# One-hot product for the last queries, merged indices and a more cautious order search in a threshold-attention kernel

## The chip, the cores and the metric

The kernel runs on one core of a Trainium2 chip. The metric is the device time of one launch in microseconds (us), of which lower is better. A run also records its span (first to last instruction of the core) and the mean clock that was granted to TensorE. The calls for runs fell on different chips; the runs of one call share a chip.

## The reference

```python
Q, K, V: (8, 12, 512, 64) float32, normal draws; threshold = 0.1
scores  = einsum('bhqd,bhkd->bhqk', Q, K) / sqrt(64)
weights = softmax(scores)                              # max subtracted, + 1e-10
weights = where(weights > threshold, weights, 0)
weights = weights / (weights.sum(-1) + 1e-10)
out     = einsum('bhqk,bhkd->bhqd', weights, V)
```

With these inputs few rows have a weight above 0.1, and those have one. Such a row of the output is one row of V; all others are zero.

## The kernel before

The output is filled with zeros. All scores are computed once in 16 bits and only **screened** (an exponential with a sum on ScalarE, or a maximum on VectorE) for rows that could hold a weight above 0.1. The few candidates of each group of four heads are then numbered, gathered, multiplied again in FP32 and judged exactly; the row of V is gathered and scattered into the output. There are 24 groups, g0 to g23. A guard sends inputs that do not fit to a general path, which these inputs never take.

```python
def do_qk(g):                     # 16-bit scores, one bank of PSUM for each head
    ...
        keep(nc.tensor.matmul(sc[:], lhsT=qk[ps, 0, hp % 2, r * P:(r + 1) * P],
                              rhs=qk[ps, 1, hp % 2, :], start=True, stop=True))
def do_screen(g, h2):
    ...
    if (h2, r) in ACT_TILES[tiles_of(q)]:
        nc.scalar.activation(junk[:], sc[:], ACTF.Exp, scale=BETA * scale / CS, accum_out=at)
    else:
        nc.vector.tensor_reduce(at, sc[:], axis=AX.X, op=ALU.max)

def do_rank(q):                   # 16 short size matmuls (for the guard), then the count of flags
    for n in range(2):
        for which in range(2):
            for r in range(SO):
                c = (1 + which) * KEY + n * C2 + 2 * r
                size = sq[:, which, n, r * P:(r + 1) * P]
                keep(nc.tensor.matmul(rk[:, c:c + 2], lhsT=size.bitcast(bf16) if which else size,
                                      rhs=heads[which][:], start=True, stop=True))
    ...                           # 8 more short matmuls with tri and ones
# then, each stage waiting for the one before:
#   keys -> one-hot (do_onehot) -> row numbers by matmul (do_idx) -> gather of Q rows ->
#   split by head -> transpose -> FP32 product (do_xqk) -> exponential -> pick -> indices ->
#   gather of V rows -> scatter to the output

def do_xone(q):
    one = small.tile([P, 1], f32)
    keep(nc.vector.tensor_scalar(one[:], kept[:, q:q + 1], ALONE, 0.0, op0=ALU.add, op1=ALU.max))
    vidx = small.tile([P, 1], i32)
    keep(nc.vector.tensor_scalar(vidx[:], one[:], 1024.0, T["rows", q][:, 3:4], op0=ALU.mult, op1=ALU.add))
    ...
def do_spare(n):                  # matmuls of nothing, in TensorE's gaps
    for _ in range(n):
        keep(nc.tensor.matmul(spare_ps[:], lhsT=warm[:, 0:P], rhs=warm[:], start=True, stop=True))
```

The order of all these steps is searched when the kernel is built. `Schedule` holds a model with a duration for each step; a random search (with a fixed seed) changes priorities, and each order is judged by the mean of four simulated runs with a little jitter:

```python
def search(self, rounds, most):
    rnd = random.Random(1)
    def price(prios):
        ...
        self.order()
        self.fill()                                   # puts spare matmuls into TensorE's gaps
        return sum(self.run(seed)[0] for seed in range(4)) / 4
    ...
sched = Schedule({"sc": SC, "sm": SM}, {"gather": 3.2, "vgather": 3.2}, 3.0, SPARE)
for op, way, spare in sched.search(800, 1.0):
    do_spare(spare)
    op[4](way[0]) if len(op[1]) > 1 else op[4]()
```

The softmax here doesn't subtract the row's maximum and nothing guards it: scores larger than these inputs give would overflow.

## Time and profile before

| | |
|---|---|
| time, median of 3 runs (range) | 251.56 us (251.01 to 252.52) |
| the profiled run: time, span, clock | 233.99 us, 232.3 us, 0.974 |
| busy: ScalarE, VectorE, TensorE | 195.7, 200.6, 205.3 us |
| last screening ends, last scatter is issued | 209.70, 225.94 us |

The row of the page that gives the granted TensorE clock in 40 equal slices (a digit is tenths of full speed) shows a run that was nearly always at full clock:

```profile
PEclk9999999999999999999997999999999999999975
```

There is one dip in the body, a window at half clock from 121.3 us, and then only the tail, where little is left for TensorE.

### The profile page before, as it was taken

Reading aid. Unit: us, or ns where it says so; the run is one execution under the profiler, and the core shown is the slowest. Engines: PE = TensorE matmul, PEld = TensorE weight load, DVE = VectorE, ACT = ScalarE, POOL = GpSimd, SP = SyncE. Lnnn points to the kernel's source line nnn. Section 1 sums busy time; section 2 is a strip of 40 time slices with the busy share of each in tenths; the row PEclk is TensorE's granted clock in tenths of the full one; section 3 lists DMA queues with packets and bytes.
Section 4 is the critical chain, followed back from the end, with each engine's and each line's share of the span. In section 5 each row is a group of like instructions: output and inputs, shape, how many; then the busy total and the mean of one; then the engine's idle time right before and its main releaser. Section 6 shows DMA issues by size and latency. Waiting matters only on the chain. (4 is left out here: it accounts for less than half of the span.)

```text
span 232.3 us, 6061 instructions
## 1 busy us (share of the span) xinstructions
PE 205.3 (88%) x1997; PEld 101.9 (44%) x2026; DVE 200.6 (86%) x574; ACT 195.7 (84%) x651; POOL 102.8 (44%) x112
## 2 busy tenths in 40 slices
PE   6999999999999799999979899999989998999700
PEld 2454553645445254444534444455535454244200
DVE  4688998999999799999987999999999999994620
ACT  2899999999998799998996998999999998992300
POOL 8120331554523633825363635344641556357440
PEclk9999999999999999999997999999999999999975
DMA  6999899496795569784954895668795300000000
GB/s 133 229 204 282 246 159 297 75 178 213 143 219 135 108 119 278 116 181 138 176 123 76 187 206 164 97 162 217 137 318 231 49 4 9 2 5 11 2 5 0
DMA packets 70737, 32.72 MB, mean 141 GB/s; under 512 B 55442, under 2 KB 67552, under 8 KB 70704
## 3 DMA queue, kind: packets, MB, share of 16 engines
q1 hardware_dynamic: 54144, 25.17, 39.7%
q0 software_dynamic: 14448, 6.61, 22.5%
q10 hardware_dynamic: 2112, 0.52, 1.2%
q8 instruction: 17, 0.28, 0.5%
q14 instruction: 16, 0.13, 0.2%
HBM read 26.74 MB, written 13.37 MB: 173 GB/s over the span
## 5 line engine op out<-in xcount | busy, mean ns | idle before, releaser
L502 ACT ACTIVATE junk<-sc 128x512 bf16<-128x512 f32 x244 | 144.1, 619 | 4.0 <-PE sc L488 3.2
L504 DVE TENSOR_REDUCE stat<-sc 128x1 f32<-128x512 f32 x140 | 93.5, 683 | 5.1 <-PE sc L488 4.7
L488 PE MATMUL sc<-qk 64*128 64x512 f16 x384 | 69.1, 384 | 4.5 <-ACT junk L502 1.8
L502 ACT ACTIVATION_READ_ACCUMULATOR junk<-sc 128x1 f32 x244 | 56.0, 229 | 0.0
L667 PE MATMUL spare_ps<-warm 128*128 128x512 bf16 x151 | 46.2, 394 | 3.2 <-DVE warm L350 2.2
L636 POOL DMA_INDIRECT out_dram<-vsel,oidx x24 | 25.9, 1078 | 52.1 <-DVE stat L504 13.9
L629 POOL DMA_INDIRECT vsel<-in_V_dram,vidx x24 | 26.8, 1118 | 25.8 <-DVE vidx L620 13.9
L563 POOL DMA_INDIRECT qsel<-in_Q_dram,idx x24 | 26.6, 1107 | 26.2 <-DVE idx L553 18.5
L488 PEld LDWEIGHTS <-qk 64*128 64x128 f16 x384 | 16.2, 93 | 36.4 <-issue 31.1
L431 PE MATMUL sc<-identity_f,k_sb 128*128 128x128 f32 x192 | 30.8, 284 | 1.5 <-ACT junk L502 0.9
L455 ACT ACTIVATE kt<-sc 128x512 f32<-128x512 f32 x48 | 29.9, 625 | 2.1 <-PE sc L431 1.9
L667 PEld LDWEIGHTS <-warm 128*128 128x128 bf16 x180 | 16.2, 102 | 29.4 <-issue 22.0
L285 POOL DMA_DIRECT2D qh<-in_Q_dram x23 | 19.1, 831 | 19.3 <-PE sc L446 15.0
L593 PE MATMUL sc<-kt,xq 128*64 128x512 f32 x96 | 26.8, 636 | 0.4 <-DVE flags L508 0.2
L472 DVE TENSOR_SCALAR qk<-kt,ksum 128x512 f16<-128x512 f32 x48 | 24.1, 501 | 3.2 <-ACT kt L455 3.2
L431 PEld LDWEIGHTS sc<-identity_f,k_sb 128*128 128x128 f32 x192 | 21.1, 142 | 11.5 <-ACT junk L502 4.4
L600 ACT ACTIVATE e<-sc 128x512 f32<-128x512 f32 x24 | 14.7, 614 | 9.2 <-PE sc L593 9.0
L547 PEld LDWEIGHTS <-oh 128*128 128x128 f16 x192 | 14.1, 164 | 10.0 <-issue 4.2
L612 DVE SCALAR_TENSOR_TENSOR pick<-e,tv,worth 128x512 f32<-128x512 f32 x24 | 17.9, 747 | 0.2
L478 DVE TENSOR_SCALAR sq<-qk 128x2048 uint16<-128x2048 uint16 x24 | 16.8, 700 | 0.0
L547 PE MATMUL sm<-row_no,oh 128*128 128x4 f16 x192 | 15.4, 202 | 1.2 <-DVE oh L536 0.5
L536 DVE TENSOR_TENSOR oh<-slot_no,keys 128x1024 f16<-128x1024 bf16 x24 | 16.4, 683 | 0.1
(75 smaller groups left out, 187.5 us busy)
## 6 DMA issues: line engine op xcount, KB each, us to landing
out_dram<-zero SPq DMA_DIRECT2D x24, 512.0 KB, 5.7
k_sb<-in_K_dram SPq DMA_DIRECT2D x94, 128.0 KB, 4.3
qh<-in_Q_dram POOLq DMA_DIRECT2D x23, 256.0 KB, 4.8
qsel<-in_Q_dram,idx POOLq DMA_INDIRECT x24, 2.7
vsel<-in_V_dram,vidx POOLq DMA_INDIRECT x24, 3.5
out_dram<-vsel,oidx POOLq DMA_INDIRECT x24, 2.6
k_sb<-in_K_dram ACTq DMA_DIRECT2D x2, 128.0 KB
first<-in_Q_dram ACTq DMA_DIRECT2D x2, 128.0 KB, 5.2
```

The costliest lines, as they stand in the source:

```text
L431: keep(nc.tensor.matmul(sc[:, r * P:(r + 1) * P], lhsT=src[:, r, :], rhs=identity_f32[:], is_transpose=True, start=True, stop=True))
L455: ins = nc.scalar.activation(kt[:], sc[:], ACTF.Copy, accum_out=ksum[:])
L472: keep(nc.vector.tensor_scalar(T["qk", hp // 2][:, 1, hp % 2, :], T["kt", hp][:], CS, T.pop(("ksum", hp))[:, 0:1], op0=ALU.mult, op1=ALU.s ...
L488: keep(nc.tensor.matmul(sc[:], lhsT=qk[ps, 0, hp % 2, r * P:(r + 1) * P], rhs=qk[ps, 1, hp % 2, :], start=True, stop=True))
L502: keep(nc.scalar.activation(junk[:], sc[:], ACTF.Exp, scale=BETA * scale / CS, accum_out=at))
L504: keep(nc.vector.tensor_reduce(at, sc[:], axis=AX.X, op=ALU.max))
L547: keep(nc.tensor.matmul(ix[:], lhsT=oh[:, c, :], rhs=row_no[:, c, :], start=(c == 0), stop=(c == C2 - 1)))
L563: keep(nc.gpsimd.indirect_dma_start(out=qsel_bufs[q % NS][:], out_offset=None, in_=Qr, in_offset=bass.IndirectOffsetOnAxis(ap=T.pop(("idx" ...
L593: keep(nc.tensor.matmul(sc[sl, :], lhsT=xq[:, sl], rhs=T.pop(("kt", 2 * q + n))[:], start=True, stop=True))
L629: keep(nc.gpsimd.indirect_dma_start(out=vsel_bufs[q % NS][:], out_offset=None, in_=Vr, in_offset=bass.IndirectOffsetOnAxis(ap=T.pop(("vidx ...
L636: s = nc.gpsimd.indirect_dma_start(out=Or, out_offset=bass.IndirectOffsetOnAxis(ap=T.pop(("oidx", q))[:, 0:1], axis=0), in_=vsel_bufs[q % ...
L667: keep(nc.tensor.matmul(spare_ps[:], lhsT=warm[:, 0:P], rhs=warm[:], start=True, stop=True))
```

## The change

It has four parts. The indices of the V gather and the scatter are merged into one VectorE operation each. For the last group alone, a one-hot matrix in FP32 and matmuls against Q rows already in SBUF take the place of the gather of Q. The search judges an order by ten jittered runs instead of four, with later landings and 1200 rounds instead of 800. And the tile for the spare matmuls is set first. The intent: less VectorE work, a shorter tail, and an order that bears delays better.

```diff
-    def run(self, seed=None, late=0.02, drift=1.0):
+    def run(self, seed=None, late=0.05, drift=1.2):
-            return sum(self.run(seed)[0] for seed in range(4)) / 4
+            return sum(self.run(seed)[0] for seed in range(10)) / 10
+    warm = consts.tile([P, SO * P], bf16)                     # moved up from further down
+    keep(nc.vector.memset(warm[:], 0.0))
-    ALONE = 8192.0
+    ALONE = 2.0 ** 23
     ...
     def do_onehot(q):
+        if q == NQ - 1:
+            oh = lpool.tile([P, C2, 2, SLOTS], f32, name="oh_last")
+            keep(nc.vector.tensor_tensor(out=..., in0=slot_no..., in1=keys..., op=ALU.is_equal))
+            T["oh", q] = oh
+            return
     def do_idx(q):
-            keep(nc.tensor.matmul(ix[:], lhsT=oh[:, c, :], rhs=row_no[:, c, :],
+            keep(nc.tensor.matmul(ix[:], lhsT=oh[:, c, :], rhs=(row_no_f32 if q == NQ - 1 else row_no)[:, c, :],
+    def do_xsel(q):
+        ...
+        for n in range(2):
+            for r in range(SO):
+                for h2 in range(2):
+                    keep(nc.tensor.matmul(xp[h2 * D:(h2 + 1) * D, n * SLOTS:(n + 1) * SLOTS],
+                                          lhsT=last_q[n][:, r, h2 * D:(h2 + 1) * D], rhs=oh[:, h2 * SO + r, n, :],
+                                          start=(r == 0), stop=(r == SO - 1)))
+        ...
     def do_xone(q):
-        keep(nc.vector.tensor_scalar(one[:], kept[:, q:q + 1], ALONE, 0.0, op0=ALU.add, op1=ALU.max))
-        keep(nc.vector.tensor_scalar(vidx[:], one[:], 1024.0, T["rows", q][:, 3:4], op0=ALU.mult, op1=ALU.add))
+        keep(nc.vector.tensor_scalar(vidx[:], kept[:, q:q + 1], T["rows", q][:, 3:4], 0.0, op0=ALU.add, op1=ALU.max))
     ...
-    sched = Schedule({"sc": SC, "sm": SM}, {"gather": 3.2, "vgather": 3.2}, 3.0, SPARE)
+    sched = Schedule({"sc": SC, "sm": SM}, {"gather": 4.0, "vgather": 4.0}, 3.0, SPARE)
-    FAR, NEAR = 6.0, 4.3
+    FAR, NEAR = 7.0, 4.5
     ...                                     # POOL steps 1.1-1.2 -> 1.3, scatter landing 3.0 -> 4.0
-        stage("idx", IDX, ["oh"], do_idx, takes=[("sm", ("ix", q))])
+        stage("idx", IDX, ["oh"] if q < NQ - 1 else ["oh", "xsel"], do_idx, takes=[("sm", ("ix", q))])
-    for op, way, spare in sched.search(800, 1.0):
+    for op, way, spare in sched.search(1200, 1.0):
```

More of the change, by code (lines that the diff above doesn't have):

```diff
@@ L279 @@
     hpool = ctx.enter_context(tc.tile_pool(name="h", bufs=2))
+    lpool = ctx.enter_context(tc.tile_pool(name="last", bufs=1))
+    last_q = {}
     fpool = ctx.enter_context(tc.tile_pool(name="first", bufs=1))
@@ L322 @@
     nc.gpsimd.iota(row_i[:], pattern=[[S, 2], [1, SO]], base=-4 * S, channel_multiplier=SO)
+    row_no_f32 = consts.tile([P, C2, 4], f32)
     row_no = consts.tile([P, C2, 4], f16)
@@ L328 @@
     nc.gpsimd.tensor_copy(row_no[:, :, 0], row_i[:])
+    nc.gpsimd.tensor_copy(row_no_f32[:], row_no[:])
+    ALONE = 2.0 ** 23
     slot_base = consts.tile([P, 4], f32)
@@ L333 @@
     nc.vector.memset(slot_base[SLOTS:P, 0:1], float(6 * S))
-    nc.vector.memset(slot_base[SLOTS:P, 3:4], float(2 * S))
-    ALONE = 8192.0
+    nc.vector.memset(slot_base[0:SLOTS, 3:4], ALONE)
+    nc.vector.memset(slot_base[SLOTS:P, 3:4], ALONE + 2 * S)
     key_i = consts.tile([P, SO, P], i32)
@@ L339 @@
     worth = consts.tile([P, SO * P], f32)
-    nc.gpsimd.tensor_scalar(worth[:], key_i[:].rearrange("p r k -> p (r k)"), 1.0 / 1024.0, -ALONE,
-                            op0=ALU.mult, op1=ALU.add)
+    nc.gpsimd.tensor_scalar(worth[:], key_i[:].rearrange("p r k -> p (r k)"), -ALONE, None, op0=ALU.add)
     heads = []
@@ L348 @@
         heads.append(one)
-    warm = consts.tile([P, SO * P], bf16)
-    nc.vector.memset(warm[:], 0.0)
     zero = consts.tile([P, 4 * SO * D], f32)
@@ L534, in do_onehot @@
     def do_onehot(q):
+        if q == NQ - 1:
+            oh = lpool.tile([P, C2, 2, SLOTS], f32, name="oh_last")
+            keep(nc.vector.tensor_tensor(
+                out=oh[:].rearrange("p c n s -> p n s c"), in0=slot_no[:].unsqueeze(1).to_broadcast([P, 2, SLOTS, C2]),
+                in1=keys[:, q, 0:KEY].rearrange("p (n c) -> p n c", n=2).unsqueeze(2)
+                    .to_broadcast([P, 2, SLOTS, C2]),
+                op=ALU.is_equal))
+            T["oh", q] = oh
+            return
         oh = work.tile([P, 2, SLOTS, C2], f16)
@@ L543, in do_idx @@
     def do_idx(q):
-        oh = T.pop(("oh", q))[:].rearrange("p n s c -> p c (n s)")
+        oh = T.pop(("oh", q))[:].rearrange("p c n s -> p c (n s)" if q == NQ - 1 else "p n s c -> p c (n s)")
         ix = mpsum.tile([P, 4], f32, name="sm", tag="sm")
         for c in range(C2):
-            keep(nc.tensor.matmul(ix[:], lhsT=oh[:, c, :], rhs=row_no[:, c, :],
+            keep(nc.tensor.matmul(ix[:], lhsT=oh[:, c, :], rhs=(row_no_f32 if q == NQ - 1 else row_no)[:, c, :],
                                   start=(c == 0), stop=(c == C2 - 1)))
@@ L580, in do_xtr, with load_last @@
                               rhs=identity_f32[:], is_transpose=True, start=True, stop=True))
+        T["xp", q] = xp
+    def load_last(n):
+        last_q[n] = lpool.tile([P, SO, 2 * D], f32, name=f"last{n}")
+        load_pair(last_q[n], Qf, NP - 2 + n)
+    def do_xsel(q):
+        xp = mpsum.tile([P, P], f32, name="sm", tag="sm")
+        oh = T["oh", q]
+        for n in range(2):
[4 more added lines that the diff above has]
+                                          start=(r == 0), stop=(r == SO - 1)))
         T["xp", q] = xp
@@ L616, in do_xone @@
     def do_xone(q):
-        one = small.tile([P, 1], f32)
-        keep(nc.vector.tensor_scalar(one[:], kept[:, q:q + 1], ALONE, 0.0, op0=ALU.add, op1=ALU.max))
         vidx = small.tile([P, 1], i32)
-        keep(nc.vector.tensor_scalar(vidx[:], one[:], 1024.0, T["rows", q][:, 3:4], op0=ALU.mult, op1=ALU.add))
-        T["one", q], T["vidx", q] = one, vidx
+        keep(nc.vector.tensor_scalar(vidx[:], kept[:, q:q + 1], T["rows", q][:, 3:4], 0.0, op0=ALU.add, op1=ALU.max))
+        T["vidx", q] = vidx
     def do_xto(q):
         oidx = small.tile([P, 1], i32)
-        keep(nc.vector.tensor_scalar(oidx[:], T.pop(("one", q))[:], T.pop(("rows", q))[:, 0:1], None, op0=ALU.max))
+        keep(nc.vector.tensor_scalar(oidx[:], kept[:, q:q + 1], 8192.0, T["rows", q][:, 0:1],
+                                     op0=ALU.add, op1=ALU.max))
         T["oidx", q] = oidx
@@ L681 @@
     RANK, IDX, XTR, XQK = pe(0.70, 0.76, 0.025), pe(0.59, 0.63, 0.008), pe(0.18, 0.30, 0.1), pe(1.0, 1.93, 0.35)
+    XSEL = pe(1.3, 2.2, 0.3)
     def add(name, ways, deps, prio, fn, takes=(), gives=()):
@@ L737 @@
         stage("key", ("DVE", 0.12, 0.25), ["rank"], do_key, gives=[("sm", ("rk", q))])
-        stage("oh", ("DVE", 0.60, 0.72), ["key"], do_onehot)
-        stage("idx", IDX, ["oh"], do_idx, takes=[("sm", ("ix", q))])
-        stage("idxev", ("DVE", 0.13, 0.25), ["idx"], do_idxev)
-        stage("rows", ("DVE", 0.07, 0.2), ["idx", "idxev"], do_rows, gives=[("sm", ("ix", q))])
-        late = FAR if q < NQ - 3 else NEAR
-        stage("gather", ("POOL", 1.2, late), ["idxev"], do_gather)
-        stage("split", ("DVE", 0.2, 0.33), ["gather", "rows"], do_split)
-        stage("xtr", XTR, ["split"], do_xtr, takes=[("sm", ("xp", q))])
-        stage("xev", [("ACT", 0.16, 0.30), ("DVE", 0.20, 0.33)], ["xtr"], do_xev, gives=[("sm", ("xp", q))])
+        if q == NQ - 1:
+            for i in range(2):
+                add(("last", i), ("DMA", 1.25, 4.0), [("qk", g0 - 24)], g0 - 24, lambda i=i: load_last(i))
+            stage("oh", ("DVE", 1.1, 1.22), ["key"], do_onehot)
+            stage("xsel", XSEL, ["oh"], do_xsel, takes=[("sm", ("xp", q))])
+            sched.ops[-1][2].extend([("last", 0), ("last", 1)])
+        else:
+            stage("oh", ("DVE", 0.60, 0.72), ["key"], do_onehot)
+        stage("idx", IDX, ["oh"] if q < NQ - 1 else ["oh", "xsel"], do_idx, takes=[("sm", ("ix", q))])
+        if q < NQ - 1:
+            stage("idxev", ("DVE", 0.13, 0.25), ["idx"], do_idxev)
+        stage("rows", ("DVE", 0.07, 0.2), ["idx", "idxev"] if q < NQ - 1 else ["idx"], do_rows, gives=[("sm", ("ix", q))])
+        late = FAR if q < NQ - 3 else NEAR
+        if q < NQ - 1:
+            stage("gather", ("POOL", 1.3, late), ["idxev"], do_gather)
+            stage("split", ("DVE", 0.2, 0.33), ["gather", "rows"], do_split)
+            stage("xtr", XTR, ["split"], do_xtr, takes=[("sm", ("xp", q))])
+        stage("xev", [("ACT", 0.16, 0.30), ("DVE", 0.20, 0.33)], ["xtr" if q < NQ - 1 else "xsel"], do_xev, gives=[("sm", ("xp", q))])
         stage("xqk", XQK, ["xev"], do_xqk, takes=[("sc", ("xs", q))])
@@ L750 @@
         stage("xpick", ("DVE", 0.70, 0.80), ["xlimit"], do_xpick)
-        stage("xone", ("DVE", 0.31, 0.43), ["xpick"], do_xone)
-        stage("xto", ("DVE", 0.12, 0.24), ["xone"], do_xto)
-        stage("vgather", ("POOL", 1.2, late), ["xone"], do_vgather)
-        stage("scatter", ("POOL", 1.1, 3.0), ["xto", "vgather", "z"], do_scatter)
+        stage("xone", ("DVE", 0.18, 0.30), ["xpick", "rows"], do_xone)
+        stage("xto", ("DVE", 0.12, 0.24), ["xpick"], do_xto)
+        stage("vgather", ("POOL", 1.3, late), ["xone"], do_vgather)
+        stage("scatter", ("POOL", 1.3, 4.0), ["xto", "vgather", "z"], do_scatter)
         if q == NC1 - 1:
```

## The prediction

> **What bounds the kernel now.** A group is a pair of head pairs; there are 24, g0 to g23. I read the busy shares first, then the groups, then the waits of ScalarE and VectorE, then the timeline of the end. From the page:
>
> ```profile
> PE 205.3 (88%) x1997; PEld 101.9 (44%) x2026; DVE 200.6 (86%) x574; ACT 195.7 (84%) x651; POOL 102.8 (44%) x112
> ...
> L502 ACT ACTIVATE junk<-sc 128x512 bf16<-128x512 f32 x244 | 144.1, 619 | 4.0 <-PE sc L488 3.2
> L504 DVE TENSOR_REDUCE stat<-sc 128x1 f32<-128x512 f32 x140 | 93.5, 683 | 5.1 <-PE sc L488 4.7
> ...
> L667 PE MATMUL spare_ps<-warm 128*128 128x512 bf16 x151 | 46.2, 394 | 3.2 <-DVE warm L350 2.2
> ```
>
> PE is busiest only on paper: 46.2 us of it are spare matmuls that fill gaps to hold the clock. The real load is the screening, shared by ScalarE (244 exponentials) and VectorE (140 maxima). The stretch from 12 us to the last screening shows both filled alike:
>
> ```profile
> 12.00:209.70 197.70, 185.75 (x1880) 93.50 (x1909) 186.08 (x499) 186.41 (x627) 87.05 (x84) 0.99 0.69 154
> ```
>
> The columns are length, then busy time of PE, weight load, VectorE, ScalarE, GpSimd, clock, DMA share. VectorE and ScalarE are each busy 94% of 197.7 us. So the **body** is bound by two balanced engines, with some 11.5 us of gaps each. The **tail** is another thing: after the last screening of g23, 22.6 us of the 232.3 us span are left, a chain of latencies. GpSimd's timeline shows it:
>
> ```profile
> 210.43 1.02 POOL L563 DMA_INDIRECT qsel<-in_Q_dram,idx  x1 [0.30 <-issue]
> 211.75 1.02 POOL L636 DMA_INDIRECT out_dram<-vsel,oidx  x1 [0.31 <-issue]
> 213.07 1.01 POOL L563 DMA_INDIRECT qsel<-in_Q_dram,idx  x1 [0.30 <-issue]
> 216.73 1.00 POOL L629 DMA_INDIRECT vsel<-in_V_dram,vidx  x1 [2.64 <-DVE oidx L625]
> 218.52 1.00 POOL L629 DMA_INDIRECT vsel<-in_V_dram,vidx  x1 [0.80 <-DVE oidx L625]
> 219.83 1.02 POOL L636 DMA_INDIRECT out_dram<-vsel,oidx  x1 [0.30 <-issue]
> 221.53 1.01 POOL L636 DMA_INDIRECT out_dram<-vsel,oidx  x1 [0.69 <-DVE oidx L625]
> 222.85 1.05 POOL L629 DMA_INDIRECT vsel<-in_V_dram,vidx  x1 [0.30 <-issue]
> 225.94 1.00 POOL L636 DMA_INDIRECT out_dram<-vsel,oidx  x1 [2.05 <-DVEq L779]
> ```
>
> These are, in turn: Q gather g22, scatter g20, Q gather g23, V gathers g21 and g22, scatters g21 and g22, V gather g23, scatter g23. Two things are to be seen. The Q gather of g23, issued at 213.07, is used by VectorE only at 216.86 (the split in the timeline), 3.8 us later. And the V gather of g23 goes out at 222.85 although its index began at 220.91 and took 0.21 us: it stood 1.7 us behind the scatter of g22. GpSimd issues in the order of the program, each indirect transfer holding it 1.3 us (1.02 plus a gap of 0.30).
>
> **What the Trainium skill says.** "VectorE: DVE Perf Modes", section on the TRN2 errata, gives (N+151)/0.96 ns for an elementwise operation at one element per cycle, and its section on the perf-mode tiers lets tensor_tensor do two per cycle only in 16 bits. The present one-hot (1024 elements, 16 bits) would be (512+151)/0.96 = 691 ns; the trace has 683, so it agrees. "FP8 and Floating Point Precision", section TensorE Precision Notes: true FP32 takes four passes. The trace has two concurrent FP32 matmuls of 512 columns in 1.08 us; four passes of 512 columns at 2.4 GHz are 0.85 us, so it fits with some fill. "DMA: Bandwidth & Descriptors", section Anatomy of one DMA, puts a fixed cost of about 2 us on a GpSimd transfer; the trace has 2.7 us (Q) and 3.5 us (V) from issue to landing for 32 KB, so a removed gather is worth more here. "Runtime: NRT & Kernel Launch" tells of some 15 us around a kernel. The profiled execution took 233.99 us, the timed ones 251.56; I take the 17.6 us as a constant (estimate) that the change doesn't touch.
>
> **The change, part by part.**
>
> *Merged indices.* Per group one VectorE operation goes (the "one" row, 148 ns); what is left are two operations that both read the kept value. In all 24 x 0.148 = 3.6 us of VectorE. By the program's order, the search also moves one more of the 1024-element copies of transposed Q from ScalarE (1.02 us) to VectorE (0.68 us). In the body, with some 21 groups finished: VectorE -3.1 +0.7 = -2.4 us, ScalarE -1.0 us. As screenings can't move between the two but the orders keep both filled alike, I take the mean, -1.7 us, over 0.94 busy: **-1.8 us**.
>
> *New order.* Ten draws in place of four, more jitter, Q and V gathers assumed to land at 4.0 us or more in place of 3.2. The trace says what this could win: in the body VectorE waits 3.0 us for Q gathers (three times) and ScalarE 5.5 us for the second product (six times). It could also lose, since a longer assumed landing delays users of data that is there already. I book **0**, with 1.5 us either way.
>
> *The warm tile first.* The spare matmuls start about 1 us earlier (now 2.16 us, held by that memset). But the first ScalarE work after the first K is the cast of the first Q at 6.91, behind a Q load that lands at 6.2. **0**. The FP32 copy of the row numbers on GpSimd is at the start too, 0.2 us, and hidden.
>
> *One-hot product for g23.* Gone for g23: the wait idx to gather to split to transpose. Added: a one-hot in FP32, (1024+151)/0.96 = 1.22 us in place of 0.68 (estimate, by the formula above); 16 FP32 matmuls of 64 columns, by passes 16 x 4 x 64 / 2.4 GHz = 1.7 us, half of it concurrent in two column halves, with weight loads about 1.4 us (estimate); 8 FP32 matmuls for the indices behind the second product, about 1.3 us in place of 0.66. Two loads of 256 KB early, hidden.
>
> Alone, g23 wins: now key to second product 210.51 to 217.89 = 7.4 us; new 0.2 + 1.2 + 1.4 + 0.3 + 0.4 for hops = 3.5 us, so nearly 4 us. But the new order of the tail does not let it have them. On PE the order is: second product g20, transpose g21, second product g21, rank g23, transpose and second product g22, then the one-hot product of g23. On GpSimd: Q gather g22, V gathers g20 and g21, scatters g20 and g21, V gather g22, **scatter g22, V gather g23**, scatter g23. From X, the end of the second product of g20, with durations of the rows and a hop of 0.1:
> ScalarE: exponential g20 to X+0.7, last screening to X+1.4, exponential g21 (behind its product, X+1.75) to X+2.6. VectorE: pick g21 (0.75) to 3.6, keys g23 3.75, vidx and oidx g21 4.05, split g22 4.3. Its gather was issued by X-0.3 and landed by X+2.6, so VectorE's place in order holds it, not the DMA. Transpose, copy, second product of g22 to 6.15, exponential 6.9, limit and pick 7.9, vidx 8.2, V gather g22 8.5, scatter g22 11.5 (3.0 later, as 218.52 to 221.53), V gather g23 12.8, scatter g23 15.9 (3.1 later, as 222.85 to 225.94). For g23: one-hot to 5.5, product from 6.15 to 7.6, second product to 9.05, exponential 9.75, rows (behind the FP32 index matmuls) 10.45, pick 11.4, oidx and vidx 11.8. So g23 is ready at about 12.1 and goes at 12.8: g22 sets the end.
> From the last screening (X+1.4) to the last scatter is then 14.5 us; now it is 209.75 to 225.94 = 16.2. **-1.7 us.** After the scatter 6.4 us follow, before and after alike.
>
> Sum: 251.56 - 1.8 - 1.7 = **248.0 us** (-1.4%).
>
> **The rivals.** (a) *g23 alone bounds the tail.* Then its 4 us count in full, plus the V gather's 1.7 us wait: 251.56 - 1.8 - 5.7 = 244.1. For it: the last chain of the profile runs through g23. Against: the order of GpSimd puts scatter g22 ahead, and g22 still has its Q gather. (b) *The saved VectorE time does not count*, as ScalarE with -1.0 us and the same waits for PE sets the body: 251.56 - 1.7 - 0.5 = 249.4. For it: 244 of 384 screenings are ScalarE's. (c) *The search's order costs.* Users placed later for assumed landings of 4 us that take 2.7, with ScalarE waiting more on PE: 3 to 4 us back, 251 to 252. Against: VectorE did wait on gathers. (d) *The new order removes the body's gaps*, say 3 of 11.5 us beside my sum: 245.
>
> **Range and chances.** My two negative terms are each uncertain by about 1 us and the order by 1.5 to 2; together some 2.4 us. So 8 in 10: 245.0 to 251.0. Faster by over 2% means below 246.5: it takes (a) or (d), 0.27. Slower by over 2% means above 256.6, 0.02. Within: 0.71.
>
> **What would show it.** VectorE's busy time falls to some 197.7 us with the "one" row gone; ScalarE's to 194.7. The last screening comes about 1.8 us earlier (208 us). From it to the last scatter's issue some 14.5 us, with g23's V gather directly behind the scatter of g22, its own index ready before. The one-hot in FP32 takes about 1.2 us, its product 1.4. I am wrong if the g23 index comes after the scatter of g22 (then PE's FP32 matmuls are the new bound), if the last screening moves by over 3 us either way (then the order search is the effect, not the operations), or if the 17.6 us beside the profile change.

## The result, and the profile after

The changed kernel took 238.89 us (median of 4 runs, 237.62 to 239.85); the kernel before 252.04 us (median of 4, 251.01 to 257.67). The ratio is 0.9488 (95% interval 0.9411 to 0.9565): faster by 5%, where I had said 1.4%. A ratio here is the mean time of one kernel's fast runs over that of the other's fast runs of the same rounds, so not quite the ratio of the medians. Executions over 1.5% slower than the fastest of the same kernel are left out of the means. The four spans after are 235.7 to 237.9 us: only some 1.9 us below the times. So there is no constant of 17.6 us beside the span.

Busy times and the largest groups of the page after, which answer to the lines of before in the prediction (columns of the groups: line, engine, operation, tiles, shapes, count, busy us, mean ns, idle time before them and what ended most of it):

```profile
PE 209.1 (88%) x2023; PEld 101.8 (43%) x2050; DVE 197.4 (83%) x550; ACT 195.9 (82%) x650; POOL 102.2 (43%) x112
...
PEclk9999999999999999999999999999999999958955
...
L507 ACT ACTIVATE junk<-sc 128x512 bf16<-128x512 f32 x244 | 144.0, 612 | 10.4 <-PE sc L493 8.0
L509 DVE TENSOR_REDUCE stat<-sc 128x1 f32<-128x512 f32 x140 | 93.7, 683 | 9.1 <-PE sc L493 5.9
```

The work is as predicted: VectorE 197.4 us (197.7 predicted), ScalarE 195.9 (194.7). But the screenings wait *more* for TensorE than in the profile of before: 8.0 us instead of 3.2 on ScalarE, 5.9 instead of 4.7 on VectorE (of 10.4 and 9.1 us of all idle time before them, 4.0 and 5.1 in before). A kernel whose profile looks worse than that of before was timed 5% faster. That is a sign that the profile of before and the times of before do not belong together.

The busy time of each engine in the body, up to the last screening (length, TensorE, weight load, VectorE, ScalarE, GpSimd, clock, DMA share, GB/s):

```profile
12.00:215.28 203.28, 188.03 (x1877) 92.02 (x1903) 182.67 (x478) 186.66 (x626) 85.21 (x84) 0.98 0.69 153
```

The last screening ends 5.6 us *later* than in the profile of before. The end of GpSimd's timeline after (start, duration, what; in brackets the idle time before it and its releaser) shows the V gathers of g20 and g21, the scatters of g20 and g21, then g22's gather and scatter and g23's:

```profile
216.41 1.00 POOL L659 DMA_INDIRECT vsel<-in_V_dram,vidx  x1 [2.71 <-DVE vidx L648]
218.91 2.64 POOL L659 DMA_INDIRECT vsel<-in_V_dram,vidx  x1 [1.50 <-DVE oidx L654]
221.86 1.03 POOL L666 DMA_INDIRECT out_dram<-vsel,oidx  x1 [0.30 <-issue]
223.69 1.00 POOL L666 DMA_INDIRECT out_dram<-vsel,oidx  x1 [0.81 <-issue]
225.00 1.03 POOL L659 DMA_INDIRECT vsel<-in_V_dram,vidx  x1 [0.30 <-issue]
228.03 1.00 POOL L666 DMA_INDIRECT out_dram<-vsel,oidx  x1 [1.99 <-DVE oks L690]
229.33 1.02 POOL L659 DMA_INDIRECT vsel<-in_V_dram,vidx  x1 [0.30 <-issue]
232.02 1.01 POOL L666 DMA_INDIRECT out_dram<-vsel,oidx  x1 [1.67 <-DMA vsel<-in_V_dram,vidx]
```

As predicted, g23's gather goes directly behind the scatter of g22, its index (written at 226.93) long ready. But from the last screening to the last scatter it is 16.7 us, not 14.5. The timelines of VectorE and TensorE show the terms (L648 at 222.63 is the index of g22; each FP32 matmul stands as two records):

```profile
218.88 1.93 DVE L542 TENSOR_TENSOR oh_last<-slot_no,keys 128x1024 f32<-128x1024 bf16 x1
...
222.63 0.21 DVE L648 TENSOR_SCALAR vidx<-kept,rows 128x1 int32<-128x1 f32 x1
...
225.75 0.16 DVE L573 TENSOR_TENSOR rows<-sm,slot_base 128x4 f32<-128x4 f32 x1 [2.79 <-PE sm L561]
225.83 0.14 DVE L635 TENSOR_SCALAR tv<-sum 128x1 f32<-128x1 f32 x1
226.01 0.75 DVE L642 SCALAR_TENSOR_TENSOR pick<-e,tv,worth 128x512 f32<-128x512 f32 x1
```

```profile
220.86 1.15 PE L608 MATMUL sm<-oh_last,last 128*64 128x64 f32 x32
...
223.76 1.95 PE L561 MATMUL sm<-row_no_f,oh_last 128*128 128x4 f32 x16
```

The one-hot in FP32 took 1.93 us (1.22 estimated), its product 1.15 (1.4), the index matmuls in FP32 1.95 (1.3). (The prediction's 2.4 GHz can be read from the trace of before: spare matmuls of 512 columns start 0.216 us apart, 2.37 columns per ns.) The row numbers stand ahead of the pick in VectorE's program, so VectorE, and with it g23's pick, waited 2.79 us for those matmuls.

That isn't what set the end, though: g23's index was there at 227.13, and its gather could go only at 229.33. What set it is g22. Its index was there at 222.84, but its V gather went only at 225.00, behind the V gather of g21, which held GpSimd for 2.64 us, and the scatters of g20 and g21. That is a wait of 2.2 us where the prediction had 0.3; from there on its steps (3.0, 1.3, 3.1) came as 3.0, 1.3 and 2.7. The long hold itself goes with the FP32 one-hot: in all five traces of the changed kernel's order and its two tail edits, this gather starts 0.03 or 0.04 us after the one-hot and takes 2.64 or 2.65 us; in the four traces of other orders of the new operations, where no V gather starts within the one-hot, no V gather takes over 1.50. No run moved the gather away from the one-hot on its own, so this is a reading of traces.

### The profile page after: what moved, and what is told of

It reads as the page before. It is cut to its first block, busy times and chain, and to the rows that moved or that the text cites.

```text
span 237.9 us, 6119 instructions
## 1 busy us (share of the span) xinstructions
PE 209.1 (88%) x2023; PEld 101.8 (43%) x2050; DVE 197.4 (83%) x550; ACT 195.9 (82%) x650; POOL 102.2 (43%) x112
## 5 line engine op out<-in xcount | busy, mean ns | idle before, releaser
L507 ACT ACTIVATE junk<-sc 128x512 bf16<-128x512 f32 x244 | 144.0, 612 | 10.4 <-PE sc L493 8.0
L493 PE MATMUL sc<-qk 64*128 64x512 f16 x384 | 73.8, 385 | 6.7 <-issue 3.9
L507 ACT ACTIVATION_READ_ACCUMULATOR junk<-sc 128x1 f32 x244 | 54.2, 222 | 0.0
L697 PE MATMUL spare_ps<-warm 128*128 128x512 bf16 x138 | 44.1, 397 | 2.6 <-DVE warm L294 1.4
L666 POOL DMA_INDIRECT out_dram<-vsel,oidx x24 | 24.9, 1039 | 47.4 <-DMA vsel<-in_V_dram,vidx 22.4
L659 POOL DMA_INDIRECT vsel<-in_V_dram,vidx x24 | 28.6, 1190 | 32.3 <-DVE vidx L648 21.1
L493 PEld LDWEIGHTS <-qk 64*128 64x128 f16 x384 | 16.7, 93 | 45.8 <-issue 38.6
L577 POOL DMA_INDIRECT qsel<-in_Q_dram,idx x23 | 24.2, 1050 | 17.2 <-DVE idx L567 10.8
L477 DVE TENSOR_SCALAR qk<-kt,ksum 128x512 f16<-128x512 f32 x48 | 23.2, 486 | 2.0 <-ACT kt L460 2.0
L697 PEld LDWEIGHTS <-warm 128*128 128x128 bf16 x165 | 14.6, 104 | 23.5 <-issue 18.8
L467 DVE COPY qk<-sc 128x1024 f16<-128x1024 f16 x21 | 14.4, 686 | 4.1 <-PE sc L451 2.0
L550 DVE TENSOR_TENSOR oh<-slot_no,keys 128x1024 f16<-128x1024 bf16 x23 | 15.7, 684 | 0.0
```

The lines of the kernel that those rows point to most:

```text
L477: keep(nc.vector.tensor_scalar(T["qk", hp // 2][:, 1, hp % 2, :], T["kt", hp][:], CS, T.pop(("ksum", hp))[:, 0:1], op0=ALU.mult, op1=ALU.s ...
L507: keep(nc.scalar.activation(junk[:], sc[:], ACTF.Exp, scale=BETA * scale / CS, accum_out=at))
L577: keep(nc.gpsimd.indirect_dma_start(out=qsel_bufs[q % NS][:], out_offset=None, in_=Qr, in_offset=bass.IndirectOffsetOnAxis(ap=T.pop(("idx" ...
L659: keep(nc.gpsimd.indirect_dma_start(out=vsel_bufs[q % NS][:], out_offset=None, in_=Vr, in_offset=bass.IndirectOffsetOnAxis(ap=T.pop(("vidx ...
L666: s = nc.gpsimd.indirect_dma_start(out=Or, out_offset=bass.IndirectOffsetOnAxis(ap=T.pop(("oidx", q))[:, 0:1], axis=0), in_=vsel_bufs[q % ...
```

## The experiments

Before the first call (e0 to e3) stood **(S)**, the old order is fragile, so that most of its runs take 250 us or more, and the new search brings the gain, and **(L)**, the prediction's own step: a launch costs 17.6 us beside the span. After it came **(D)**: what the time before is depends on the chip; on one kind it is some 236 us, on the other some 251, and the change gains much on the second kind only. Within D, three theories say what gains on the second kind: **(O)** the new order, **(P)** the new operations, **(C)** chance: an order happens to suit or not. These letters hold from e6 on. In e1 to e3, O stands for the new operations; in e4 and e5, C says that where and when before was timed made the gap, and P is the prediction's sum.

**Kernel before again.** No edit.

> The kernel before, unchanged, to see its own spread and a second profile. Theory S (the order that the old search chose is fragile: small delays change which waits hold, and most executions lose about 17 us against the one that was profiled): most executions at 250 to 253 us with a span some 2 us below, a few near 234; a profile of a 251 us execution shows the extra time as idle time of ScalarE and VectorE behind PE in the body, with the granted clock lower in some slices. Theory L (launch overhead): the spans are near 232 in every execution and only the time around them is 17 us longer.

On chip 3 it took 236.16 us (median of 6, 232.10 to 238.34) and 235.85 (11 runs) under its other name; ratio 0.9927 (0.9825 to 1.003). Spans 230.5 to 239.0 us, 1.6 us below the times. So L is refuted: here the times agree with the first profile. S fails as well: none of these 17 runs took over 241 us, where it had most at 250 to 253. The difference of the two names, 0.7%, shows the noise.

**One part alone: the warm tile first.** Edit: only those two lines moved.

> The kernel before with only the warm tile written first, so that the spare matmuls start some 1 us earlier; the order is the same. Theory W (the start of PE decides whether the clock is up in the body): near 239 us. Theories S and O (search, operations): 250 to 253 us, as before.

236.21 us, ratio 1.0016 (0.9919 to 1.0113). Nothing to be seen within some 1%, as predicted.

**One part alone: the new search, operations of before.**

```diff
-    def run(self, seed=None, late=0.02, drift=1.0):
+    def run(self, seed=None, late=0.05, drift=1.2):
 ...                                  (all the changed settings of the search, no changed operation)
```

> The kernel before with only the new settings of the order search (ten draws, more jitter, later landings, 1200 tries); all operations are the old ones. Theory S: 240 to 244 us, that is nearly all of the gain. Theory O (operations: merged indices and the one-hot product bring it): 249 to 252 us.

235.17 us on chip 3, ratio 1.0005 (0.9935 to 1.0074): nothing on this kind of chip.

**The new operations with the old settings of the search.** The reverse edit, made to the changed kernel.

> The changed kernel with the old settings of the order search. Theory S: 246 to 252 us, since the order is again chosen from four draws with little jitter. Theory O: 237 to 241 us, as the changed kernel.

239.07 us (235.06, 239.00, 239.15, 240.55) on chip 3; no ratio could be given. Inconclusive.

**The changed kernel again, and before for a trace of its own.** No edits.

> The changed kernel, unchanged, in the same rounds on one chip as the kernel before. In the first set of runs the kernel before stood at 232 to 241 us, not at 251.6 as in the times quoted with it. Theory C (the 13 us between the quoted times come from where and when the kernel before was timed): 237 to 240 us for the changed kernel, and the kernel before beside it at 233 to 241, so no gain or a small loss. Theory D (the kernel before breaks down on some chips or sessions, and the changed order is what holds up): 237 to 240 us, and the kernel before beside it at 250 us or more if the chip is such a one. Theory P (the arithmetic of the prediction, -3.5 us): 231 to 234 us beside 236.

> The kernel before once more, for a trace on the same chip as the run of the changed kernel. Theory C: a span of 231 to 236 us. Theory D on a chip of the slow kind: a span near 250 us, with Q and V gathers landing later than the 2.7 and 3.5 us of the first profile.

Chip 10, of the other kind: the changed kernel took 240.04 us, before 251.25 (median of 11, 249.62 to 256.22), ratio 0.951 (0.9443 to 0.9577). The gain is real and repeats. And now there is a trace of before with the time that the prediction was given (252.31 us, span 250.6). The same stretch, 60 to 90 us, of the first profile of before:

```profile
60.00:90.00 30.00, 27.81 (x294) 13.74 (x297) 28.18 (x76) 27.38 (x93) 11.08 (x12) 1.00 0.74 155
```

and of before on chip 10:

```profile
60.00:90.00 30.00, 25.57 (x229) 10.97 (x234) 24.14 (x67) 22.31 (x76) 11.08 (x12) 0.89 0.55 115
```

ScalarE did 5 us less work in the same 30 us, at a clock of 0.89. Its granted clock falls to half from 80.5 to 87.3 us and again from 199.9 us on, with screenings still to do:

```profile
PEclk9999999999999599999999999999999957988975
```

As both traces are of one program, I could set the n-th instruction of each engine against its twin. Before on chip 10 falls behind in steps, not evenly: it is about 2 us behind by 63 us, loses 2.7 more at 79 and 4.6 at 200, is 14.4 behind at the end of the last screening and 18.3 at the end. At each large step in the body VectorE and ScalarE wait for TensorE's semaphore, none waits for a DMA. The largest step, on TensorE and then on VectorE and ScalarE (timelines of each engine; "remote" stands where the profile finds no instruction behind the update that ended a wait, and both instructions wait on TensorE's semaphore):

```profile
193.82 0.54 PE L521 MATMUL sm<-heads,sq 128*128 128x2 f16 x16
...
194.49 0.39 PE L488 MATMUL sc<-qk 64*128 64x512 f16 x2
...
195.35 0.61 PE L488 MATMUL sc<-qk 64*128 64x512 f16 x4
200.67 0.61 PE L488 MATMUL sc<-qk 64*128 64x512 f16 x2 [4.71 <-ACT junk L502]
```

```profile
199.91 0.69 DVE L504 TENSOR_REDUCE stat<-sc 128x1 f32<-128x512 f32 x1 [4.56 <-remote]
```

```profile
199.93 0.60 ACT L502 ACTIVATE junk<-sc 128x512 bf16<-128x512 f32 x1 [4.47 <-remote]
```

The reader sees a circle that makes no sense at first: the score matmuls have records from 194.49 and 195.35 us, but the two engines that need them start at 199.9, and TensorE's next matmul waits for those. The trace of semaphores resolves it: TensorE's semaphore has no recorded update between 193.88 and 199.14 us. Eight matmuls that make an update end in this gap by their records, the last at 195.96, and eight updates come from 199.14 to 200.06. The Trainium skill, "Perfetto Trace Analysis", section Tensor Engine Instruction, says that the start in a profile is when an instruction begins to fetch its data, that the end is only estimated, and that the semaphore moves when PSUM has acknowledged the writes. The case agrees: what is late by 4 us is the completion, and no TensorE record shows it. I call this a **freeze**. After it TensorE is at half clock for 10.2 us from 199.9: the skill, "TensorE: Matmul & The Clock Gate", Part 1, tells of half clock after an idle window of 3.4 us, and the half-clock windows here are of 3.4, 6.8 and 10.2 us. So a freeze can cost twice. The TensorE instruction fetches (16 KB each) took 0.9 to 1.9 us on both kinds of chip, and none was under way in the gap (the nearest at 191.3 and 210.3); they are not the cause.

**Both halves, the changed kernel, and another seed, on one chip.** The seed is the smallest change of an order that I could think of:

```diff
-        rnd = random.Random(1)
+        rnd = random.Random(2)
```

> The kernel before with only the new order search, on another draw of the chip. On a chip where before takes about 251 us: theory O (the gain on that chip is the order, which avoids the freezes of TensorE's completions and the cold clock after them) expects 239 to 242 us, ratio about 0.95 to 0.96; theory P (the gain is the new operations: shorter tail, less VectorE work) expects 249 to 252, ratio about 1.0; theory C (chance: any order differs by several us on that chip) gives no number, but then the seed run below moves by over 5 us too. On a chip where before takes about 236 us all three expect 234 to 237.

> The changed kernel with the old settings of the order search. Where before takes about 251 us: theory O expects 247 to 251 us, theory P expects 239 to 242. Where before takes about 236 us: 235 to 239, as it did the first time (235.06 to 240.55).

> The changed kernel. Where before takes about 251 us: 238 to 242, ratio about 0.95, as twice already. Where before takes about 236 us: if the gain is only in what that chip does to the kernel before, the changed kernel is within 2% of it there, 233 to 238 us; if it is a gain of the kernel everywhere, 224 to 228 us (ratio about 0.95).

> The kernel before with another seed of its random search, nothing else: same operations, another order. Theory C (an order that suits the chip by chance) expects it to differ from before by over 5 us where before takes about 251 us, either way; theories O and P expect 249 to 253 there. Where before takes about 236 us: 234 to 238.

Chip 14, of the first kind (before: 235.70 us, 7 runs). New search 234.77, ratio 0.9987 (0.9918 to 1.0056); new operations 236.47, 1.0052 (0.9983 to 1.0121); other seed 235.67, 0.9975 (0.9882 to 1.0069); the changed kernel 233.12, **0.9913 (0.9832 to 0.9995)**. So on this kind of chip the change gains about 1%, some 2 us, in four runs on one chip. Neither half shows a gain alone, though the interval of the new search reaches as far. Body and tail of the changed kernel here:

```profile
12.00:208.96 196.96, 191.08 (x1905) 91.76 (x1905) 181.80 (x478) 186.04 (x625) 85.09 (x84) 0.99 0.71 158
```

```profile
217.95 1.04 POOL L659 DMA_INDIRECT vsel<-in_V_dram,vidx  x1 [0.30 <-issue]
220.97 1.00 POOL L666 DMA_INDIRECT out_dram<-vsel,oidx  x1 [1.98 <-DVE ok L810]
222.27 1.02 POOL L659 DMA_INDIRECT vsel<-in_V_dram,vidx  x1 [0.30 <-issue]
224.73 1.01 POOL L666 DMA_INDIRECT out_dram<-vsel,oidx  x1 [1.43 <-DMA vsel<-in_V_dram,vidx]
```

The last screening ends at 208.96 us (208 predicted; 209.70 in the first profile of before), the last scatter comes 15.8 us later (16.2 before), and the end 5.9 us after that (6.4). The 0.7 us of the body are no proof: in two more traces of before's order on this kind (chip 3) the last screening ends at 211.5 and 211.7 us.

**The same parts on the second kind, and a tail edit.** The fourth kernel is the changed one with the row numbers of g23 moved behind its pick, and the scatter of g22 behind the V gather of g23.

> The kernel before with only the new order search. So far it ran on two chips where before takes some 236 us, and was the same there. Where before takes about 251 us: theory O (the gain there is the new order) expects 239 to 242 us; theory P (the new operations) 249 to 252. Where before takes about 236: 234 to 236 again, and nothing new.

> The changed kernel with the old settings of the order search. Where before takes about 251 us: theory O expects 247 to 251, theory P 239 to 242. Where before takes about 236: 235 to 239 again.

> The kernel before with another seed of its search. Where before takes about 251 us: theory C (any other order moves it by chance) expects it to lie over 5 us from before; theories O and P 249 to 253. Where before takes about 236: 234 to 238 again.

> The changed kernel with two places swapped after the search, the rest of the order as it is: the row numbers of the last group behind its pick on VectorE (the pick waited 1.2 us behind them, which wait for the FP32 index matmuls), and the last V gather ahead of the scatter of the group before it (it stood 2.6 us in that line). In the third trace of the changed kernel the last scatter is issued 15.8 us after the last screening; here I expect 13.0 to 14.0. Of that the end of the kernel should get 1.0 to 1.5 us, as the branch at the end waits for the scatter of the group before: 231.5 to 232.5 us where before takes about 236 (ratio 0.985), and 237 to 240 where it takes about 251.

Chip 7, of the second kind (before: 252.43 us, 23 runs). The new search alone took **253.52** us, ratio 1.0111 (1.0063 to 1.0158). The new operations alone took **252.60**, 1.0105 (0.9979 to 1.023). Neither O nor P holds: each half leaves before as slow as it was. Another seed of the *old* search, nothing else changed, took **244.96** (241.05 to 247.22), ratio 0.973 (0.9508 to 0.9952); a gain of some 7 us from nothing, whose size two fast runs leave wide. That is theory C. The three orders' traces have half-clock windows in the body, before its last 3 us, in different places (the first from 58.0 and 153.6 us, the second from 91.4, 152.9, 173.3 and 200.7, the third from 138.8, 193.4 and 203.6). The fourth took 240.19, 0.9632 (0.953 to 0.9733), near the changed kernel's times on this kind, and missed its expectation: the last scatter came 17.4 us after the last screening, not 13.0 to 14.0. Its edit was at fault: the row numbers did move behind the pick, but in the built program the scatter still stood ahead of the gather. The edit puts the gather ahead in the search's plan; building turned the two around, for a reason that I did not find.

**The changed kernel with another seed; the short matmuls taken away and doubled; the tail edit mended.** The two largest steps on chip 10 in the body, at 79 and 200 us, came right behind the runs of short matmuls of a rank group (the 16 of L521 above). So theory **(B)**: freezes come from such runs. In the few-sizes kernel two matmuls stand for sixteen; the guard then looks at less, the result here is the same (the tile `heads` is widened to fit):

```diff
-        for n in range(2):
-            for which in range(2):
-                for r in range(SO):
-                    ...
+        for which in range(2):
+            size = sq[:, which, 0, 0:P]
+            keep(nc.tensor.matmul(rk[:, (1 + which) * KEY:(2 + which) * KEY],
+                                  lhsT=size.bitcast(bf16) if which else size,
+                                  rhs=heads[which][:], start=True, stop=True))
```

In the double-sizes kernel each of the sixteen is issued twice. In the last kernel the row numbers stand behind the pick, and an explicit edge holds the gather ahead of the scatter:

```diff
         keep(s)
+        if q == NQ - 2:
+            tc.add_manual_dep(s.ins, T["vg", NQ - 1].ins.name, <no semaphore>, reason="the last gather first")
```

> The changed kernel, all of it, with another seed of its order search. Where before takes about 251 us: theory C (what an order is worth there is chance) expects anything from 238 to 254 us and most likely over 3 us from the 239.5 of the changed kernel; theory I (it takes the new search and the new operations together, and then it holds) expects 238 to 242. Where before takes about 236: 232 to 236 by all theories.

> The kernel before in its own order, but with 2 in place of 16 of the short size matmuls of each group (the guard against large inputs then looks at less; the result for these inputs is the same). Theory B (TensorE's completions freeze behind dense runs of short matmuls) expects clearly less where before takes about 251 us: 240 to 246; if the runs of short matmuls have nothing to do with it, 249 to 252. Where before takes about 236: 234 to 236.

> The kernel before in its own order with each of the 16 short size matmuls of a group issued twice, same result. TensorE has 24 x 0.4 = 10 us more to do (estimate from 0.40 us for 16 in the trace), of which I expect 2 to 5 us in the time, as TensorE has spare work to give but not at those places: 238 to 241 where before takes about 236. Theory B expects clearly more than that on top where before takes about 251: 262 or more; without it 253 to 257.

> The tail swap that e13 was meant to be: there the scatter of the group before still stood ahead of the last V gather in the built program; here an explicit edge puts the gather first, and the row numbers of the last group stand behind its pick. From the last screening to the last scatter 13.0 to 14.0 us (third trace of the changed kernel: 15.8). Where before takes about 236: 231.5 to 232.5 us, ratio 0.985 (the changed kernel had 0.9913). Where it takes about 251: 237 to 239.

Chip 5, again of the second kind (before: 251.35 us, 7 runs, its fast ones 247.08 to 249.22).

*Other seed of the changed kernel:* 248.36 us (244.69 to 248.83), and its **result was wrong** (relative error 0.119). So the time is only a hint: it lies over 8 us above the changed kernel on this kind of chip, against theory I (both halves together, and then it holds) and for C. Why the result was wrong I could not find out. Every run of the changed kernel in its own order was right.

*Few sizes:* **239.41** us (238.69 to 239.44, and one run of 246.45), ratio 0.9648 (0.9469 to 0.9827), with the order of before. Most of what this kind of chip costs before is gone. The clock and the stretch from 60 to 90 us show it:

```profile
PEclk9999999999999999999999999999999997999955
```

```profile
60.00:90.00 30.00, 26.91 (x226) 11.78 (x229) 28.12 (x77) 27.14 (x92) 13.12 (x14) 1.00 0.75 153
```

ScalarE is back at 27.14 us busy of 30, as in the first profile (27.38). The last screening ends at 213.44 us instead of 224.07.

*Double sizes:* 257.47 us, ratio 1.0421 (1.0204 to 1.0639). B had expected 262 or more, the other side 253 to 257: between the two. The last screening, at 225.89 us, is only 1.8 us later than in before on chip 10, so twice the short matmuls did not make twice the freezes. B is therefore not shown. Taking the matmuls away also shifts all of TensorE's timing, and C says that any such shift may move the time by several us, here too. Beyond that, the few-sizes kernel has not run on the first kind of chip, so what of its gain is plain saved work is not known.

*Gather first:* 238.90 us (239.77, 239.04, 238.75, and one of 234.32); no ratio. GpSimd's last six transfers: scatters g20 and g21, V gathers g22 and g23, scatters g22 and g23:

```profile
225.24 1.04 POOL L659 DMA_INDIRECT vsel<-in_V_dram,vidx  x1 [0.30 <-DVE tv L635]
226.93 1.01 POOL L659 DMA_INDIRECT vsel<-in_V_dram,vidx  x1 [0.64 <-DVE ok L694]
228.24 1.03 POOL L667 DMA_INDIRECT out_dram<-vsel,oidx  x1 [0.30 <-issue]
229.62 1.00 POOL L667 DMA_INDIRECT out_dram<-vsel,oidx  x1 [0.35 <-DMA vsel<-in_V_dram,vidx]
```

The last screening ended at 215.34 us, so the last scatter now comes 14.3 us later instead of 16.7 on this kind of chip (13.0 to 14.0 expected). The end follows it by 7.2 us instead of 5.9, so about 1.1 of the 2.4 us should reach the time, too little for four runs to prove. I could not show that it beats the changed kernel.

**Freezes counted in all twenty traces.** Counted is each stretch of over 2 us in the body without a recorded update of TensorE's semaphore, in which a matmul that makes one had ended, by its record, at least 1 us before the next update. The nine traces of the first kind hold one such stretch between them; each of the eleven of the second kind (the first one of the changed kernel among them, by its times) holds 3 to 10. A lost record (see below) can stretch such a gap, but not one at whose end another engine had waited. None of these kernels is free of freezes there: before has 7, few sizes 5, the changed kernel 4 and 3. They differ in whether anyone waits. Where a freeze ended (within 1.2 us), VectorE or ScalarE had been idle for over 0.8 us four times in before, nine times with the new search, six with the new operations, three times and once in the changed kernel, never with few sizes, and two to five times in the others. That fits C, by which an order decides who waits, but the count doesn't rank the kernels strictly (three also in the other seed of the change, with 248 us), and it does not tell what makes the freezes.

A rival stands untested: the recording. On the second kind semaphore records are missing as well. Of TensorE's, VectorE's and ScalarE's updates 586, 487 and 337 are recorded in the first profile of before, and 528, 427 and 293 in its trace on chip 10; all eleven traces of the second kind lack such records, and none of the nine others does to any extent. Every run of the experiments has a span and a clock on record, so each was traced. Whether freezes and slow times would be there without recording, no run tells. Nor was any chip met in two calls, so that it is the chip and not the hour that makes the two kinds is not shown either.

All of it in one table (median us; ratio to before of the same call):

| kernel | chips where before takes some 236 | chips where it takes some 251 |
|---|---|---|
| before | 235.85; 235.70 | 252.04; 251.25; 252.43; 251.35 |
| the change | 233.12 (0.9913) | 238.89 (0.9488); 240.04 (0.951) |
| new search alone | 235.17 (1.0005); 234.77 (0.9987) | 253.52 (1.0111) |
| new operations, old search | 239.07 (none); 236.47 (1.0052) | 252.60 (1.0105) |
| before, other seed | 235.67 (0.9975) | 244.96 (0.973) |
| the change, other seed | not run | 248.36 (wrong result) |
| before, few sizes / double sizes | not run | 239.41 (0.9648) / 257.47 (1.0421) |
| the change with a tail edit | not run | 240.19 (0.9632); 238.90 (none) |

## Why the prediction was wrong

**The step that failed is the last sentence of the part on the skill: "I take the 17.6 us as a constant (estimate) that the change doesn't touch."** It is not a constant and not beside the span: in every run whose span is on record the time is 1.5 to 2.0 us above it. The profile was of a run in which before takes some 234 us, the times of runs in which it takes some 251. So those 17 us belong inside the span. Where a trace of such a run was taken (chip 10), the largest steps are freezes of TensorE's completions and the half clock behind them, which the profile in my hands did not show. I then subtracted gains read from one kind of run from a time of the other kind.

**"New order: 0, with 1.5 us either way"** was right for one kind of chip (1.0005 and 0.9987 for the new search alone) and far too narrow for the other, where five orders of nearly the same work took 239 to 253 us. My list of signs had named both errors ("if the last screening moves by over 3 us either way", "if the 17.6 us beside the profile change"), but the range gave them no room.

**The body.** The bound was not contradicted on the first kind: VectorE and ScalarE have the most work besides TensorE's spare matmuls, and the last screening came 0.7 us earlier than in the first profile, where I had said 1.8. On the second kind the body's steps are waits for TensorE's completions, which no share of busy time shows. Most of the 5% comes from there: the last screening ends at 215.3 and 217.9 us in the changed kernel against 224.1 before, that is 6.2 to 8.8 us of the 9.9 to 12.7 between the spans. Another 3.3 to 3.5 us come from the tail, which in before took 20.2 us on chip 10.

**The tail.** The mechanism was right (the V gather of g23 goes behind the scatter of g22, its index ready before), the size too good: 15.8 us on the first kind, 16.7 on the second, instead of 14.5. The mis-sized term is the wait of g22's V gather in GpSimd's line: 0.3 us in the sum, 2.2 and 2.3 measured, behind a V gather of g21 that held GpSimd for 2.64 and 2.65 us and the scatters of g20 and g21. The FP32 one-hot (1.93 for 1.22) and the FP32 index matmuls (1.95 for 1.3) were mis-sized too, but g23's index was there 2.2 us before its gather could go; they were not what set the end, unless by the hold of that V gather.

**The rivals.** Rival (d), an order that removes the body's gaps, comes closest, but the gaps that went are not those that I had seen. Rival (a) is refuted by the line of g23's gather behind the scatter of g22; (b) and (c) were sums on the wrong base, and neither 249.4 nor 251 came. **Warm tile first: 0** held on the first kind (1.0016, within some 1%).

On the kind of chip of my profile the sum came near: -1.4% predicted, -0.9% measured (0.9913, interval 0.9832 to 0.9995). That is in part luck. Between the two traces of that kind the body gave 0.7 us of 1.8 and the tail 0.5 of 1.7, and 0.4 came after the last scatter, where I had expected no change. What stays open: what freezes TensorE's completions on the second kind of chip, whether runs of short matmuls or the recording provoke it, and why engines wait for it least in the one order of the change. What is shown is that the time is inside the span, that neither half of the change carries the gain by itself, and that a mere other seed moves the time there by some 7 us (0.5 to 4.9%).

## What to carry to other kernels

When a profile's span does not fit the times beside it, find out why before predicting anything: it may be the trace of a run in another condition, and every wait read from it is then a wait of that condition. When a result is due to an order found by random search, test it with other seeds and on more than one chip before crediting the change, and check the result again for each order, as one here was wrong. And where engines wait for a TensorE whose records look done, look at the semaphore's updates, not at the matmuls' bars, and count whether all of them were recorded.

## What the Trainium skill lacked or had wrong

- "Runtime: NRT & Kernel Launch", The ~15µs preamble/postamble breakdown: the page isn't shown wrong, but no such overhead is in the time measured here; the times were 1.5 to 2.0 us above the spans in all runs that have both. I misapplied the page to a gap of 17.6 us that lay inside the span.
- No page that I found tells that one single-core program can take 236 us on some chips (3, 14) and 251 us on others (10, 7, 5) in all its runs (medians).
- No page that I found tells of TensorE completions that stop for some 5 us while the matmuls' records go on (no TensorE semaphore update from 193.88 to 199.14 us), or of a tenth of the updates missing from a trace (528 recorded instead of 586). "Perfetto Trace Analysis", Tensor Engine Instruction, explains why the matmuls' records hide a late completion.
- "VectorE: DVE Perf Modes", section on the TRN2 errata: its (N+151)/0.96 ns, given for an FP32 add, would be 1.22 us for the one-hot of 1024 elements with bf16 inputs and FP32 output (estimate); it took 1.91 to 1.94 us in nine traces. This one-hot also writes its output with strides, which the formula has no term for; no run told type and strides apart. The one-hot with a 16-bit output written in order took 0.68 us, near the 0.69 of the formula at two elements per cycle.
